# A second Strassen level for the first product of six pairs of convolution cells

## The chip, the cores and the metric

The kernel runs on one core of one Trainium2 chip. The metric is the time of one execution on the device, in microseconds. Five engines work side by side, each through its own queue in order: TensorE (PE in the profile, with its weight loads as PEld), VectorE (DVE), ScalarE (ACT), GpSimd (POOL) and SyncE (SP), which issues nearly all DMAs.

## The reference, cut to what matters

One layer of a decoder trunk on a sequence of 1024 tokens of width 1024, in float32. The part that matters here is the combined input projection of the normalised input `h` (1024 x 1024):

```python
h = rms_norm(x, norm_mix_g[i])
proj = jnp.einsum('bsd,dc->bsc', h, w_in[i])
(q, k, v, z_a, gk_low, cb, cc, xc, z_c, g_a, g_c) = jnp.split(proj, idx, axis=-1)
...
u = causal_dwconv(cc * xc, conv_w[i])
y_c = jnp.einsum('bsc,cd->bsd', (cb * u) * jax.nn.silu(z_c), w_branch_c[i])
```

Each of `cc`, `xc`, `z_c` and `cb` is 1024 columns wide.

## The kernel before, in words

Every large matrix product is cut into *cells*. A cell makes 256 output columns for all 1024 tokens, from a 1024 x 256 block of weights, with one level of Strassen's scheme (seven products in place of eight). The tokens' matrix `h` is cut into quarters, and `hres` holds the seven operands that `h` gives (`hres[0]` to `hres[6]`, each 128 partitions x 4 x 512), made once and kept. A cell streams its own side: `load` fetches the weight quarters (`raw0` to `raw3`, from a ring of 8 tiles), and `prep` makes product k's operand from them on VectorE (the sums are tiles called `T`, from a ring of 4).

Products are made nearly exact in float32 by splitting each operand in two: `split` writes the high part with a ScalarE cast (`hi`) and the low part with a VectorE subtraction (`lo`), and `mm3` then makes three matmuls (hi·hi, hi·lo, lo·hi). The cells' operands lie in a ring of 8 such pairs (`RING = 8`). One product is 4 steps of the contraction x 3 = 12 matmuls whose moving operand is 512 columns wide. A cell uses three PSUM banks, X, Y and V: product 0 goes to X and is copied to Y (ScalarE); product 1 goes to V; products 2, 4 and 6 add to Y, 3 adds to X, 5 adds to V; VectorE and ScalarE take the four output quarters away (`cons`).

There are 40 cells on the weights of `h`, the outputs and the gates, and the sixteen *convolution cells* `cc0, xc0, zc0, cb0, cc1, ... cb3` are among them (four for each group of 256 channels). They run one after the other, all seven products of one cell before the next (`single`). Other cells run in pairs, in which the products of two cells alternate (`pairs`, in the order `PAIR` = 0, 1, 2, 3, 5, 4, 6). `run_groups` walks the list of products, and before it runs one it asks for the loads of the next 14 and the preparation of the next 7.

Nothing of this is issued at once. `Flow` records all operations; `put_in_order` then sets the order on each engine by a list schedule of its own with assumed costs and due times (the main matmuls keep the order of the program), and `emit` issues them. So every instruction of the profile stands at line 507, and instructions are told apart by the names of their tiles: `cc1X<-h0hi,cc1lo` is a matmul of product 0 of cell cc1. Work that fills gaps is woven in by `weave` and `tick` (two ticks for each product): during the convolution cells this is `weights`, which prepares the weights of the last two projections, eight tiles `wt` of 1 MB in two buffers.

After the convolution cells come the gate cells `ga` and `gc` (in pairs, their product 0 was made at the start) with the attention woven in, then `yc`, `ya`, `out` and `gt`. The products 4 and 6 of the last cell `gt3` are made by halves, with a moving operand of 256 columns (`by_halves`).

Of the kernel before, what the change touches and what calls it, by code (L numbers as in the profile page):

```python
# [9 lines left out]
F32 = mybir.dt.float32  # L10
F32R = mybir.dt.float32r
# [3 lines left out]
ALU = mybir.AluOpType  # L15

P = 128
# [8 lines left out]
RING = 8  # L26
# [492 lines left out]
def kernel(  # L519
# [16 lines left out]
    nc = Flow(tc)  # L536
    PS = bass.MemoryType.PSUM
    tt = nc.vector.tensor_tensor
# [3 lines left out]
    def f(ap):  # L542
        return ap.bitcast(F32)
# [85 lines left out]

    def finish_woven():  # L630
        while woven:
            tick()


    def bank(cell, n):
        return psm.tile([P, 512], F32, tag=f"m{3 * cell.set + n}", name=f"{cell.name}{'XYV'[n]}")
# [92 lines left out]

    class Cell:  # L730


        def __init__(self, name, side, src, res, cons, prods=ORDER, begin=None, s1=None, u2=None, s5=None, fresh=(), mixed=False):
            self.name, self.side, self.src, self.res, self.cons = name, side, src, res, cons
            self.prods, self.begin, self.after = list(prods), begin, None
            self.get = {"u2": u2, "s5": s5}
            self.s1, self.seed, self.ready, self.halves = s1, None, lambda k: True, None
            self.raw, self.ring, self.order = [None] * 4, {}, None
            self.steps, self.fresh = ring_steps(name, side, self.raw, fresh, mixed), fresh

        def load(self, k):
            for n in NEED[self.side][k]:
                if self.raw[n] is None and not (self.fresh and k == 1 and n == 3):
                    self.raw[n] = bp.tile([P, 4, P], F32, tag="raw", name=f"{self.name}raw{n}", bufs=8)
                    load(self.raw[n], self.src[n])
            if k == 1 and self.s1 is not None and self.seed is None:
                self.seed = bp.tile([P, 512], F32, tag="raw", name=f"{self.name}s1", bufs=8)
                load(self.seed, self.s1)

        def prep(self, k):  # L750
            if k not in self.ring:
                self.load(k)
                self.ring[k] = self.steps[k]()

        def product(self, k, acc, start):
            self.prep(k)
            shi, slo = self.ring[k]
            rhi, rlo = self.res[k]
            for kt in range(4):
                nc.side = False  # L760
                mm3(acc, shi[:, kt, :], slo[:, kt, :], rhi[:, kt, :], rlo[:, kt, :], start and kt == 0, kt == 3)
                nc.side = True
                if kt % 2 == 1:
                    tick()
# [26 lines left out]
        def run(self, k):  # L791
            if k == self.prods[0]:
                if self.begin:
                    self.begin()
                self.Y = None
            if k == 0:
                self.X = bank(self, 0)
                self.product(0, self.X, True)
                self.Y = bank(self, 1)
                nc.scalar.copy(self.Y, self.X)  # L800
            elif k == 1:
                if self.Y is None:
                    self.Y = bank(self, 1)
                    nc.scalar.copy(self.Y, self.seed)
                self.V = bank(self, 2)
                self.product(1, self.V, True)
                self.c22 = self.taken("s5", self.V)
            elif k == 2:
                self.product(2, self.Y, False)
                self.c12 = self.taken("u2", self.Y)  # L810
                if self.halves:
                    self.Z = psm.tile([P, 512], F32, tag=f"m{3 * (1 - self.set)}", name=f"{self.name}Z")
                    nc.scalar.copy(self.Z[:, 256:], self.Y[:, 256:])
            elif k == 3:
                self.product(3, self.X, False)
                self.cons(0, 0, self.X)
            elif k == 5:
                self.product(5, self.V, False)
                tt(self.c12, self.V, self.c12, op=ALU.add)
                self.cons(0, 1, self.c12)  # L820
            elif k in (4, 6) and self.halves:
                self.by_halves(k)
            elif k == 4:
                self.product(4, self.Y, False)
                tt(self.c22, self.Y, self.c22, op=ALU.add)
                self.cons(1, 1, self.c22)
            elif k == 6:
                self.product(6, self.Y, False)
                self.cons(1, 0, self.Y)
            if self.after:  # L830
                self.after(k)

    def line_up(groups):
        for n, g in enumerate(groups):
            for s, c in enumerate(g):
                c.set = (s if len(g) > 1 else n) % 2
        return [(g[s], k) for g in groups
                for s, k in (g[0].order or [(s, k) for k in g[0].prods for s in range(len(g))])]

    def single(cs):  # L840
        return [[c] for c in cs]

    def pairs(cs):
        for c in cs:
            c.prods = [k for k in PAIR if k in c.prods]
        return [list(cs[n:n + 2]) for n in range(0, len(cs), 2)]

    def run_groups(groups, more=(), ahead=6):


        todo = line_up(groups)
        seq = todo + line_up(more)
        for n, (c, k) in enumerate(todo):
            for reach, what in ((RING + ahead, Cell.load), (RING - 1, Cell.prep)):
                for cc, kk in seq[n:n + reach]:
                    if not cc.ready(kk):
                        break
                    what(cc, kk)
            c.run(k)

    ep = phase("ev")
# [75 lines left out]
    hres = [None] * 7  # L937
# [10 lines left out]
    with phase("prep0") as pool:  # L948
# [75 lines left out]
        at = [0]  # L1024
# [155 lines left out]
    with phase("v", [ph["prep0"]]) as qp:  # L1180
# [76 lines left out]
        qks = []  # L1257
# [4 lines left out]
    with phase("qk", [ph["v"]]) as qp:  # L1262
# [63 lines left out]
        vp = phase("conv", [ph["qk"]])  # L1326
        convs = []
        for g in range(4):
            t, u = [], []
# [35 lines left out]
            for m, cons in (("cc", cc_cons), ("xc", xc_cons), ("zc", zc_cons), ("cb", cb_cons)):  # L1365
                convs.append(Cell(f"{m}{g}", "B", W[f"{m}{g}"], hres, cons, begin=cc_begin if m == "cc" else None))

        run_groups(single(qks), single(convs[:2]))

    with vp:  # L1370
        def weights(vp):


            for w in range(2):
                for kt in range(4):
                    t = vp.tile([P, 4, 512], F32, tag="wt", name=f"wt{w}_{kt}", bufs=2)
                    load(t, wb[w][:, :, kt, :].rearrange("n p c -> p n c"))
                    yield 14
                    b11, b12, b22, b21 = (t[:, n] for n in range(4))
                    if w:  # L1380
                        for n, q in enumerate((b11, b12, b22, b21)):
                            k = kt + 4 * (n >= 2)
                            act(q, q, AF.Copy, scale=gple[:, k:k + 1])
                            if n != 1:
                                store(wtd[w][4 + (n + 1) // 2][:, kt, :], q)
                    tt(b11, b12, b11, op=ALU.subtract)
                    yield 2
                    tt(b12, b22, b12, op=ALU.subtract)
                    yield 2
                    tt(b22, b22, b11, op=ALU.subtract)  # L1390
                    yield 2
                    tt(b21, b21, b22, op=ALU.subtract)
                    for n, q in enumerate((b11, b22, b12, b21)):
                        store(wtd[w][n][:, kt, :], q)
                    yield 4

        gas, gcs = ([Cell(f"{m}{c}", "B", W[f"{m}{c}"], hres, gate_cons(c, bias, dst), prods=(1, 2, 4, 5, 6),
                          s1=s1d[n + c]) for c in range(4)]
                    for n, m, bias, dst in ((0, "ga", bga, gad), (4, "gc", bgc, gcd)))
        weave(weights(vp), 10)  # L1400
        run_groups(single(convs), pairs(gas[:2]))
        finish_woven()

    def attend(hp, ap):
# [456 lines left out]
```

## Time and profile before

| | before |
|---|---|
| median of 3 runs | 1080.68 us (1080.42 to 1080.77) |
| profiled execution, its own time | 1080.98 us |
| its span, first to last instruction | 1079.2 us |
| granted TensorE clock | 0.998 |
| PE / DVE / ACT busy, share of the span | 99% / 81% / 56% |

The page shows one profiled execution. Busy times are sums over the span; the chain that ended last is followed back from the last instruction; a matmul's listed duration runs on after the next one has begun, so the pace of matmuls is read from their starts, or from the chain, which gives consecutive matmuls of one tile with their count and the time they took together.

### The profile page before, as it was taken

Reading aid. Unit: us, or ns where it says so; the run is one execution under the profiler, and the core shown is the slowest. Engines: PE = TensorE matmul, PEld = TensorE weight load, DVE = VectorE, ACT = ScalarE, POOL = GpSimd, SP = SyncE. Lnnn points to the kernel's source line nnn. Section 1 sums busy time; section 2 is a strip of 40 time slices with the busy share of each in tenths; the row PEclk is TensorE's granted clock in tenths of the full one; section 3 lists DMA queues with packets and bytes.
Section 4 is the critical chain, followed back from the end, with each engine's and each line's share of the span. In section 5 each row is a group of like instructions: output and inputs, shape, how many; then the busy total and the mean of one; then the engine's idle time right before and its main releaser. Section 6 shows DMA issues by size and latency. Waiting matters only on the chain.

```text
span 1079.2 us, 14643 instructions
## 1 busy us (share of the span) xinstructions
PE 1069.8 (99%) x4881; PEld 890.8 (83%) x4881; DVE 868.8 (81%) x1353; ACT 605.5 (56%) x1095; POOL 45.5 (4%) x83
## 2 busy tenths in 40 slices
PE   9999999999999999999999999999999999999997
PEld 7887887888888888888888888888888888888886
DVE  6998567678997976857757788887999978889896
ACT  6778538656543455333333367675757635466555
POOL 0000000000000000000000012110000000011021
PEclk9999999999999999999999999999999999999999
DMA  9973564457766598221222689989486878799963
GB/s 315 365 233 105 173 209 142 152 196 233 227 213 220 197 316 266 74 98 49 74 83 69 227 275 310 332 297 333 174 310 234 283 228 297 233 347 339 301 225 139
DMA packets 144828, 239.96 MB, mean 222 GB/s; under 512 B 12016, under 2 KB 57328, under 8 KB 141808
## 3 DMA queue, kind: packets, MB, share of 16 engines
q1 hardware_dynamic: 144608, 238.76, 65.6%
q8 instruction: 38, 0.62, 0.3%
q14 instruction: 38, 0.31, 0.1%
q10 hardware_dynamic: 144, 0.26, 0.1%
HBM read 158.24 MB, written 80.74 MB: 221 GB/s over the span
## 4 chain that ended last, share of the span: by engine, by line
PE 98%; ACT 1%; DVE 0%; issue 0%; POOL 0%; ACTq 0%; DVEq 0%
PE vY L507 3%; PE zaY L507 3%; PE pe L507 2%; PE vX L507 2%; PE zaV L507 2%; PE vV L507 2%; PE op L507 2%; PE zaX L507 2%; PE kv L507 1%; PE ga2Y L507 1%; PE ga0Y L507 1%; PE ga1Y L507 1%; PE ga3Y L507 1%; PE cb3Y L507 1%; PE gc0Y L507 1%; PE xc1Y L507 1%
## 5 line engine op out<-in xcount | busy, mean ns | idle before, releaser
L507 ACT ACT_TABLE_LOAD x20 | 25.7, 1283 | 1.1 <-PEq L1850 0.7
L507 ACT ACTIVATE junk<-x 128x512 bf16<-128x512 f32 (+1 forms) x30 | 18.0, 600 | 12.2 <-DVE x L507 11.8
L507 DVE TENSOR_TENSOR wt<-wt 128x512 f32<-128x512 f32 x32 | 21.7, 687 | 0.3
L507 DVE SCALAR_TENSOR_TENSOR u<-t,vec,u 128x1024 f32<-128x1024 f32 x16 | 20.4, 1278 | 0.0
L507 POOL MEMSET t<- 128x2 f32 x8 | 0.8, 99 | 442.6 <-DMA qkd<-kk 243.7
L507 POOL TENSOR_SCALAR rg<-ms 128x1 f32<-128x1 f32 x8 | 6.4, 796 | 261.4 <-ACT junk L507 261.2
L507 ACT ACTIVATE junk<-op 128x256 bf16<-128x256 f32 x32 | 12.2, 380 | 3.2 <-PE op L507 3.0
L507 ACT CAST S<-S 128x512 fp32r<-128x512 f32 x14 | 8.7, 619 | 9.2 <-PE op L507 8.6
L507 ACT ACTIVATE og<-op,or 128x256 f32<-128x256 f32 x32 | 13.3, 470 | 0.1
L507 ACT ACTIVATE oq<-oq,vec 128x512 f32<-128x512 f32 x20 | 13.1, 715 | 0.0
L507 PE MATMUL pe<-wpehi,pThi 128*128 128x512 f32 x32 | 13.0, 405 | 0.0
L507 PE MATMUL pe<-wpelo,pThi 128*128 128x512 f32 x32 | 13.0, 405 | 0.0
L507 PE MATMUL pe<-wpehi,pTlo 128*128 128x512 f32 x32 | 12.8, 401 | 0.0
L507 PE MATMUL op<-v,aTh 128*128 128x256 f32 x64 | 12.8, 283 | 0.0
L507 DVE TENSOR_TENSOR szl<-og,szl 128x512 f32<-128x512 f32 x16 | 11.0, 688 | 2.1 <-ACT og L507 2.1
L507 POOL TENSOR_TENSOR or<-or,mhalf 128x2 f32<-128x2 f32 x16 | 12.2, 765 | 1.3
L507 DVE SCALAR_TENSOR_TENSOR hq<-hq,vec,rt 128x512 f32<-128x512 f32 x16 | 11.2, 742 | 0.6 <-PE rt L507 0.6
L507 DVE SCALAR_TENSOR_TENSOR S<-S,dds,kv 128x256 f32<-128x256 f32 x24 | 10.4, 475 | 1.5 <-PE kv L507 1.4
L507 DVE TENSOR_TENSOR x<-x,pe 128x512 f32<-128x512 f32 (+1 forms) x18 | 11.2, 629 | 0.3
L507 DVE STREAM_TRANSPOSE oT<-szl 128x512 f32<-128x512 f32 x16 | 11.3, 705 | 0.1
L507 DVE TENSOR_TENSOR u<-u,s 128x512 f32<-128x512 f32 x16 | 10.9, 689 | 0.3
L507 ACT ACTIVATE wt<-wt,vec 128x512 f32<-128x512 f32 x16 | 10.5, 715 | 0.6 <-issue 0.6
(2919 smaller groups left out, 4109.4 us busy)
## 6 DMA issues: line engine op xcount, KB each, us to landing
wtd<-wt SPq DMA_DIRECT2D x44, 256.0 KB, 3.6
wt<-in_wb_dram SPq DMA_DIRECT2D x8, 1024.0 KB, 7.3
v<-vd SPq DMA_DIRECT2D x16, 512.0 KB, 6.1
wgq<-wtd SPq DMA_DIRECT2D x7, 1024.0 KB, 6.5
qk<-qkd SPq DMA_DIRECT2D x12, 512.0 KB, 6.1
vraw<-in_wv_dram SPq DMA_DIRECT2D x20, 256.0 KB, 4.2
zaraw<-in_wv_dram SPq DMA_DIRECT2D x20, 256.0 KB, 3.9
uq<-ud SPq DMA_DIRECT2D x5, 1024.0 KB, 7.3
```

What stands on the lines that cost most here:

```text
L507: o.call(*[place(a) for a in o.args], **{k: place(a) for k, a in o.kw.items()})
```

## The change: what it does

The sixteen convolution cells run in pairs (cc, xc) and (zc, cb). For the last six pairs (groups 1 to 3) the two products 0 of a pair are made together by a new class `Deep`. Both products have the same `hres[0]` on one side, so together they are one product of 512 x 512 weights (two cells' `raw0`, 256 columns each) with 512 x 512 of `h`; `Deep` makes it by a second Strassen level: seven quarter-size products, each 2 steps of the contraction x 3 = 6 matmuls with a moving operand of 256 columns. `h`'s side of the seven operands (`turned`) is made once by `quarters`, woven into the first convolution pairs; one of them is written over a quarter of `hres[0]` once the last cell that needs the plain `hres[0]` (cb0) has made its product 0. The pair's side is made in `Deep.prep` (four half-width sums, four splits, four slots of the ring of 8).

`Deep.run` has four steps, which `line_up` puts between the last products of the pair before: step 0 (two quarter products), product 4 of the second cell, step 1 (two), product 6 of the first cell, step 2 (one), product 6 of the second cell, step 3 (two). Sums of quarter products are made in PSUM: the step's result is copied from one half bank to others by ScalarE (`u`, `X`, and `dw` to SBUF in step 0; `u`'s second half in step 1; `X`'s second half in step 2), and VectorE writes the second cell's X as `u` + `dw` after step 2; the next quarter products add to these. At the end both X are copied to Y, as before.

The `wt` tiles get one buffer instead of two. Cells that are not of these six pairs keep their product 0.

```diff
@@ run (class Cell)
             if k == self.prods[0]:
                 if self.begin:
                     self.begin()
-                self.Y = None
...
+    class Deep:
+        def __init__(self, pair, turned, pool):
+            self.pair, self.turned, self.pool, self.ring = pair, turned, pool, []
+            for c in pair:
+                c.deep, c.prods = self, [k for k in c.prods if k]
+        slots = 4
...
+        def prep(self, k):
...
+            t = [bp.tile([P, 4, P], F32, tag="T", name=f"{name}S{m}", bufs=4) for m in range(2)]
+            s1, s2, s3, s4 = (t[m][:, n:n + 2, :] for m in range(2) for n in (0, 2))
+            tt(s3, a[:, 0:2, :], b[:, 0:2, :], op=ALU.subtract)
+            tt(s1, b[:, 0:2, :], b[:, 2:4, :], op=ALU.add)
+            tt(s2, s1, a[:, 0:2, :], op=ALU.subtract)
+            tt(s4, a[:, 2:4, :], s2, op=ALU.subtract)
+            a11, a12 = put("A", a)
+            s1, s2 = put("S", t[0])
+            s3, s4 = put("T", t[1])
+            a22, = put("B", b[:, 2:4, :])
+            self.ring = [a11, s3, s2, a12, s1, s4, a22]
+
+        def product(self, n, acc, start):
+            shi, slo = self.ring[n]
+            rhi, rlo = self.turned[n]
+            for kt in range(2):
+                nc.side = False
+                mm3(acc, shi[:, kt, :], slo[:, kt, :], rhi[:, kt, :], rlo[:, kt, :], start and kt == 0, kt == 1)
+                nc.side = True
+            tick()
+
+        def run(self, k):
+            self.prep(k)
+            a, b = self.pair
+            left, right = slice(0, 256), slice(256, 512)
+            if k == 0:
+                self.w = pso.tile([P, 512], F32, tag="o", name=f"{a.name}w", bufs=2)
+                self.product(0, self.w[:, left], True)
+                self.product(1, self.w[:, right], False)
+                self.u = pso.tile([P, 512], F32, tag="o", name=f"{a.name}u", bufs=2)
+                a.X = bank(a, 0)
+                nc.scalar.copy(self.u[:, left], self.w[:, left])
+                nc.scalar.copy(a.X[:, left], self.w[:, left])
+                self.d = self.pool.tile([P, 256], F32, tag="dw", name=f"{a.name}dw")
+                nc.scalar.copy(self.d, self.w[:, right])
+            elif k == 1:
+                self.product(2, self.u[:, left], False)
+                nc.scalar.copy(self.u[:, right], self.u[:, left])
+                self.product(3, a.X[:, left], False)
+            elif k == 2:
+                self.product(4, self.u[:, right], False)
+                nc.scalar.copy(a.X[:, right], self.u[:, right])
+                b.X = bank(b, 0)
+                tt(b.X.rearrange("p (n c) -> p n c", n=2), self.u.rearrange("p (n c) -> p n c", n=2),
+                   self.d[:, None, :].to_broadcast([P, 2, 256]), op=ALU.add)
+            else:
+                self.product(5, a.X[:, right], False)
+                self.product(6, b.X[:, left], False)
+                for c in self.pair:
+                    c.Y = bank(c, 1)
+                    nc.scalar.copy(c.Y, c.X)
...
@@ line_up
+            if g[0].deep:
+                for n in range(4):
+                    todo.insert(len(todo) - 3 + n, (g[0].deep, n))
...
@@ the convolution cells
-        run_groups(single(qks), single(convs[:2]))
+        convs = pairs(convs)
+        run_groups(single(qks), convs[:1])
...
-                    t = vp.tile([P, 4, 512], F32, tag="wt", name=f"wt{w}_{kt}", bufs=2)
+                    t = vp.tile([P, 4, 512], F32, tag="wt", name=f"wt{w}_{kt}", bufs=1)
...
+        def quarters(turned):
+            hi, lo = hres[0]
+            th, tl = (vp.tile([P, 3, 2, 256], F32R, name=f"turned{w}") for w in "hl")
...
+            t3 = put(2, apart(2, (1, 1), (0, 1)))
+            yield 1
+            t = apart(0, (0, 1), (0, 0))
+            t1 = put(0, t)
+            yield 1
+            t = less((1, 1), t)
+            t2 = put(1, t)
+            while wide_last[-1].Y is None:
+                yield 1
+            t4 = put(3, less((1, 0), t))
+            b11, b21, b22 = ((at(hi, *a), at(lo, *a)) for a in ((0, 0), (1, 0), (1, 1)))
+            turned += [b11, t3, t2, b21, t1, b22, t4]
+
+        turned = []
+        wide_last = convs[1]
+        for g in convs[2:]:
+            Deep(g, turned, vp)
         weave(weights(vp), 10)
-        run_groups(single(convs), pairs(gas[:2]))
+        weave(quarters(turned), 20)
+        run_groups(convs, pairs(gas[:2]))
```

In `quarters`, `apart` is three VectorE operations on 128 x 512, `less` is two, and each `put` there is one split. In `run_groups` the reach of loads and preparations counts a `Deep` as four slots.

More of the change, by code (lines that the diff above doesn't have):

```diff
@@ L730 @@
     class Cell:
+        slots = 1
         def __init__(self, name, side, src, res, cons, prods=ORDER, begin=None, s1=None, u2=None, s5=None, fresh=(), mixed=False):
@@ L737, in __init__ @@
             self.s1, self.seed, self.ready, self.halves = s1, None, lambda k: True, None
-            self.raw, self.ring, self.order = [None] * 4, {}, None
+            self.raw, self.ring, self.order, self.Y, self.deep = [None] * 4, {}, None, None, None
             self.steps, self.fresh = ring_steps(name, side, self.raw, fresh, mixed), fresh
@@ L831, in run, with ready, load, put @@
                 self.after(k)
+    class Deep:
[4 more added lines that the diff above has]
+        slots = 4
+        def ready(self, k):
+            return True
+        def load(self, k):
+            for c in self.pair:
+                c.load(0)
+        def prep(self, k):
+            if self.ring:
+                return
+            self.load(k)
+            a, b = (c.raw[0] for c in self.pair)
+            name = self.pair[0].name + self.pair[1].name
+            def put(what, src):
+                hi = bp.tile([P, 4, P], F32R, tag="whi", name=f"{name}{what}hi", bufs=RING)
+                lo = bp.tile([P, 4, P], F32R, tag="wlo", name=f"{name}{what}lo", bufs=RING)
+                n = src.shape[1]
+                split(hi[:, 0:n, :], lo[:, 0:n, :], src)
+                return [(hi[:, m:m + 2, :], lo[:, m:m + 2, :]) for m in range(0, n, 2)]
+            t = [bp.tile([P, 4, P], F32, tag="T", name=f"{name}S{m}", bufs=4) for m in range(2)]
[44 more added lines that the diff above has]
+                self.product(6, b.X[:, left], False)
+                for c in self.pair:
+                    c.Y = bank(c, 1)
+                    nc.scalar.copy(c.Y, c.X)
@@ L836, in line_up @@
                 c.set = (s if len(g) > 1 else n) % 2
-        return [(g[s], k) for g in groups
-                for s, k in (g[0].order or [(s, k) for k in g[0].prods for s in range(len(g))])]
+        todo = []
+        for g in groups:
+            if g[0].deep:
+                for n in range(4):
+                    todo.insert(len(todo) - 3 + n, (g[0].deep, n))
+            todo += [(g[s], k) for s, k in (g[0].order or [(s, k) for k in g[0].prods for s in range(len(g))])]
+        return todo
     def single(cs):
@@ L853, in run_groups @@
         for n, (c, k) in enumerate(todo):
-            for reach, what in ((RING + ahead, Cell.load), (RING - 1, Cell.prep)):
-                for cc, kk in seq[n:n + reach]:
-                    if not cc.ready(kk):
+            for reach, what in ((RING + ahead, "load"), (RING - 1, "prep")):
+                met = set()
+                for cc, kk in seq[n:]:
+                    if cc not in met:
+                        reach -= cc.slots
+                    if cc.slots > 1:
+                        met.add(cc)
+                    if reach < 0 or not cc.ready(kk):
                         break
-                    what(cc, kk)
+                    getattr(cc, what)(kk)
             c.run(k)
@@ L1399, with apart, less, put @@
                     for n, m, bias, dst in ((0, "ga", bga, gad), (4, "gc", bgc, gcd)))
+        def quarters(turned):
+            hi, lo = hres[0]
+            th, tl = (vp.tile([P, 3, 2, 256], F32R, name=f"turned{w}") for w in "hl")
+            left, right = slice(0, 256), slice(256, 512)
+            at = lambda t, i, j: t[:, 2 * i:2 * i + 2, (left, right)[j]]
+            tile = lambda n: bp.tile([P, 2, 256], F32, tag="T", name=f"turned{n}", bufs=4)
+            def apart(i, a, b):
+                t, o = tile(i), tile("o")
+                tt(t, f(at(hi, *a)), f(at(hi, *b)), op=ALU.subtract)
+                tt(o, f(at(lo, *a)), f(at(lo, *b)), op=ALU.subtract)
+                tt(t, t, o, op=ALU.add)
+                return t
+            def less(a, t):
+                o = tile("d")
+                tt(o, f(at(hi, *a)), t, op=ALU.subtract)
+                tt(o, o, f(at(lo, *a)), op=ALU.add)
+                return o
+            def put(n, src):
+                h, l = (th[:, n], tl[:, n]) if n < 3 else (at(hi, 0, 1), at(lo, 0, 1))
+                split(h, l, src)
+                return h, l
+            t3 = put(2, apart(2, (1, 1), (0, 1)))
[14 more added lines that the diff above has]
+            Deep(g, turned, vp)
         weave(weights(vp), 10)
-        run_groups(single(convs), pairs(gas[:2]))
+        weave(quarters(turned), 20)
+        run_groups(convs, pairs(gas[:2]))
         finish_woven()
```

## Prediction

> **What bounds the kernel now.** I read the page's head first, then the chain, then the convolution stage by windows.
>
> ```profile
> span 1079.2 us, 14643 instructions
> PE 1069.8 (99%) x4881; PEld 890.8 (83%) x4881; DVE 868.8 (81%) x1353; ACT 605.5 (56%) x1095; POOL 45.5 (4%) x83
> PEclk9999999999999999999999999999999999999999
> PE 98%; ACT 1%; DVE 0%; issue 0%; POOL 0%; ACTq 0%; DVEq 0%
> ```
>
> TensorE is busy for 99% of the span and carries 98% of the chain that ended last, at the full clock all the way. No other engine is near. So a microsecond of matmuls taken out is a microsecond off the end, as long as TensorE doesn't have to wait in exchange; and it has no wait now that could be removed. The stage that is changed, in the windows view (columns: stretch, length, then the busy time of PE, PEld, DVE, ACT, POOL with their instructions, clock, DMA share, GB/s), with three stretches beside it:
>
> ```profile
> 313.00:618.00 305.00, 305.00 (x1349) 252.62 (x1349) 225.26 (x341) 123.34 (x213) 1.42 (x10) 1.00 0.45 150
> 351.00:389.00 38.00, 38.00 (x170) 31.47 (x169) 34.45 (x53) 16.89 (x28) 0.20 (x2) 1.00 0.69 232
> 760.00:850.00 90.00, 90.00 (x399) 74.59 (x398) 86.57 (x114) 60.91 (x91) 0.00 (x0) 1.00 0.71 244
> ```
>
> The sixteen convolution cells run from 313 to 618 us. TensorE is busy for 305.00 of 305.00 us, VectorE for 225.26 (74%), ScalarE for 123.34 (40%). The third row is a stage of the same kind with pairs of cells, where VectorE is busy for 86.57 of 90 us (96%) and TensorE still never waits.
>
> **What the matmuls save.** The pace of wide matmuls is in the chain (start, length, what, how many), that of narrow ones in the timeline of the last cell, whose products 4 and 6 are made by halves (48 matmuls of 256 columns in a row; three of them, with the last wide one ahead):
>
> ```profile
> 389.61 2.72 PE cc1X L507 x12
> 1065.22 0.39 PE L507 MATMUL gt3V<-wg5hi,gt3lo 128*128 128x512 f32 x1
> 1065.45 0.28 PE L507 MATMUL gt3Y<-wg4hi,gt3hi 128*128 128x256 f32 x1
> ...
> 1069.63 0.28 PE L507 MATMUL gt3Y<-wg6hi,gt3lo 128*128 128x256 f32 x1
> 1069.75 0.28 PE L507 MATMUL gt3Z<-wg6hi,gt3hi 128*128 128x256 f32 x1
> ```
>
> A product 0 is 12 matmuls in 2.72 us, 0.2267 us each. From 1065.45 to 1069.63 lie 35 starts of narrow ones: 4.18 / 35 = 0.1194 us each, more than half of 0.2267. A pair loses 24 wide matmuls (24 x 0.2267 = 5.44 us) and gains 7 x 6 = 42 narrow ones. At 0.1194 these are 5.02 us: 0.42 us saved for a pair, 2.55 us for six. But there the narrow ones stand in one long row. In the changed kernel they stand in four groups of 12, 12, 6 and 12 between wide ones, and this the trace shows too, where the attention's narrow matmuls lie among the gate cells' wide ones:
>
> ```profile
> 669.27 1.45 PE op L507 x12
> 670.72 2.52 PE ga2Y L507 x11
> 673.24 2.72 PE ga3Y L507 x12
> ```
>
> Twelve narrow ones took 1.45 us (0.1208 each), and the eleven wide ones behind them 2.52 us where 11 x 0.2267 = 2.49: a change of width costs some 0.03 us (the next twelve are back at 2.72). So a pair costs 42 x 0.1208 + 4 x 0.03 = 5.07 + 0.11 = 5.18 us, 0.26 us less than 5.44; six pairs save 1.55 us. These are the two ends of the matmuls' gain, 1.55 and 2.55 us; I take the first, rounded to 1.6, since it is the row with the new placement.
>
> The Trainium skill ("TensorE: Matmul & The Clock Gate", back-to-back issue gap) gives N / 2.4 + 2.5 ns for a warm matmul. By it 24 wide ones would be an estimated 5.18 us and 42 narrow ones 4.59, six pairs 3.6 us, and the kernel would end near 1077.1; the rows here show 13 ns beside the columns, not 2.5, and they decide.
>
> **What the other engines get, and what hides it.** Durations, from groups of instructions of the stage and of the last cell (`xcount | busy, mean ns | idle before`):
>
> ```profile
> L507 DVE TENSOR_TENSOR xc1lo<-xc1T,xc1hi 128x512 fp32r<-128x512 f32 x4 | 2.8, 690 | 1.8 <-ACT xc1hi L507 1.8
> L507 DVE SCALAR_TENSOR_TENSOR u<-t,vec,u 128x1024 f32<-128x1024 f32 x16 | 20.4, 1278 | 0.0
> L507 DVE TENSOR_SCALAR u<-t,vec 128x1024 f32<-128x1024 f32 x8 | 6.0, 748 | 0.0
> L507 ACT CAST cc2hi<-cc2T 128x512 fp32r<-128x512 f32 x4 | 2.5, 622 | 6.9 <-PE cb1V L507 3.7 <-PE cb1X L507 3.2
> L507 ACT ACTIVATE s<-zc1u 128x512 f32<-128x512 f32 x1 | 0.6, 635 | 1.6 <-DVE zc1u L507 1.6
> L507 ACT COPY gt3Z<-gt3Y x1: 381/381/381, 1060.7 to 1060.7; 128x256 f32<-128x256 f32 x1
> L507 DVE TENSOR_TENSOR gt3s<-gt3Z,gt3s x1: 421/421/421, 1068.7 to 1068.7; 128x256 f32<-128x256 f32 x1
> ```
>
> For a pair VectorE gets four half-width sums (4 x 0.42), one and a half splits more than the two that product 0 had (0.69 + 0.42) and the sum that writes the second X (0.69): 3.5 us. `quarters` adds ten sums and four splits once, 14 x 0.69 = 9.7 us. Six pairs and `quarters` are 30.6 us, and VectorE comes to 256 of some 303 us, 84%. ScalarE gets five copies of 256 (5 x 0.38) and one and a half casts (1.0): 2.9 us for a pair, 20 us with the four casts of `quarters`, 143 of 303 us. Both stay below what the 760 to 850 stretch carries without a wait, so as sums they cost nothing. The tight place is 351 to 389 us, where VectorE has 34.45 of 38 us already and `quarters` and the first pair's preparation (13 us) come down. Its cover is the lead of the preparation:
>
> ```profile
> 371.45 0.69 DVE L507 TENSOR_TENSOR cc1lo<-cc1raw,cc1hi 128x512 fp32r<-128x512 f32 x1
> ```
>
> cc1's first operand is ready 18 us before TensorE starts on cc1 (389.61 above). VectorE may fall back by what it lacks (34.45 + 13 - 38 = 9 us) and still be ahead. If that cover were used up before, it would cost up to those 9 us, once.
>
> The lead does get shorter. A `Deep` holds four of the ring's eight slots until step 3, so the operands around it have 3 to 4 products of lead (some 7 to 9 us) where they had seven (19 us). A cast and a `lo` need 0.62 + 0.69 us after their slot is free. I count nothing for it.
>
> **The new waits.** TensorE waits four times for results of its own that come back through ScalarE: step 1 on step 0, step 2 on step 1, step 3 on step 2, and products 2 on step 3. Between any two lies a full product, 2.72 us. The order of the changed program shows what stands ahead of each copy. Steps 1 and 2 are easy: behind step 0 ScalarE has a cast, a sigmoid (or a copy) and then the copy that is waited for, 0.62 + 0.64 + 0.38 = 1.6 of 2.72 us plus step time. Step 3 is the tightest. In the pairs (cc, xc) the copy of X's second half waits for VectorE's 512-wide sum. From the end of the product ahead of step 2: 0.16 us for the last matmul's result (0.39 - 0.23, from the rows above), a cast 0.62, a `lo` 0.69, the sum 0.69, the copy 0.38 = 2.5 us; TensorE comes to step 3 after 0.72 + 2.72 = 3.44 us. Margin 0.9 us. In the pairs (zc, cb) VectorE has the convolution of xc ahead of that sum (0.75 + 1.28 us): counted from the end of step 1 it is 0.16 + 0.62 + 0.69 + 0.42 + 0.69 + 0.75 + 1.28 + 0.69 + 0.69 = 6.0 us, and the quarter product that reads it starts 2.72 + 0.72 + 2.72 + 0.72 = 6.9 us after that point. Margin 0.9 us again. So no wait, in each of six pairs, but by less than the length of two instructions.
>
> **What else moves.** `wt` has one buffer: SyncE waits for the four stores of one tile before it issues the next load, and the cells' loads queue behind that.
>
> ```profile
> wtd<-wt SPq DMA_DIRECT2D x44, 256.0 KB, 3.6
> wt<-in_wb_dram SPq DMA_DIRECT2D x8, 1024.0 KB, 7.3
> ```
>
> A load is issued, and 14 ticks (about 19 us) later its tile is used; 3.6 + 7.3 = 11 us fit in. The cells' loads behind are held up by 3.6 us, and are needed several products later: nothing, and 3.6 us for a tile if that lead were gone. The order of conv cells in pairs adds no matmul. At the end of the stage zc3 is finished beside cb3, but zc3's last chain (sigmoid and two products, 2.2 us) fits into cb3's last product (2.72 us). POOL has nothing to do with it.
>
> **Sum.** 1080.98 us is the profiled execution's own time (span 1079.2 + 1.8 around it); less 1.6 that is 1079.4. The median of the runs is 0.3 us below that execution, so I forecast 1080.68 - 1.6 = 1079.1 us. With both ends of the matmul cost: 1078.1 to 1079.1; with a few tenths of waits up to 1079.6.
>
> **Rivals.** Some 0.2% (2.16 us) is what a measurement of this kernel can tell from no change, so faster means below 1078.5 and slower above 1082.8.
>
> *Narrow matmuls at their best pace.* If the change of width costs nothing here, six pairs save 2.55 us: 1078.1. For it: the 48 in a row at 0.1194, and that the 0.03 us behind them was seen only in the attention stage, where other things differ. Against it: each of those groups shows it. If width alone set the pace (2.72 / 24 = 0.113), it would be 4.1 us and 1076.6; the row at 0.1194 speaks against that.
>
> *The weight loads become the bound.* 42 loads stand where 24 stood, and a load is listed with 0.19 us:
>
> ```profile
> L507 PEld LDWEIGHTS gt3Z<-wg4hi,gt3hi 128*128 128x128 f32 x4 | 0.8, 192 | 0.0
> ```
>
> One after the other they would take 42 x 0.192 = 8.1 us, 2.6 us more than before: 1096.5. Against it: in that very row of 48 a matmul started each 0.119 us, so loads overlap.
>
> *Waits eat the gain.* At 0.1 to 0.5 us for a pair the time lies between 1079.7 and 1082.1, near no change.
>
> *Step 3 comes late (slower).* If VectorE or ScalarE is one instruction of 1.28 us further behind than the order suggests, each pair's step 3 waits 0.4 us (1.28 - 0.9); if it is two (a convolution in front of the sum and a late `lo`, 2.2 us), 1.3 us. Six times 1.3 less 1.6 is +6.2: 1086.9. It turns to slower from a wait of 0.63 us for a pair ((2.16 + 1.6) / 6). For it: the margins of 0.9 us, the ring with half its lead, a VectorE that must wait for TensorE before nearly each `lo`. Against it: VectorE at 96% made no wait at 760 to 850.
>
> **How the numbers follow.** Forecast (1.6 us saved, 1078.5 to 1079.6): 0.50. Best pace: 0.25, width alone 0.02. Waits eat the gain: 0.10. Step 3 late: 0.12; weight loads: 0.01. Faster takes the best pace, width alone and a little of the forecast's low end, 0.30; slower 0.13; within 0.2% the rest, 0.57. The range 1078.0 to 1082.0 holds the forecast, the best pace and nearly all of the eaten gain; outside are step 3 late, the weight loads and width alone.
>
> **What would show it.** TensorE still busy for all of the stage, and the next gate cell's first product some 1.6 us earlier than at 618 us. In the chain, groups of 12 `w`, 12 `u` and `X`, 6 `u`, 12 `X` at 1.45, 1.45, 0.72 and 1.45 us, and the wide products behind them at 2.72 to 2.75. VectorE near 84% of the stage. I am wrong if the waits list TensorE behind ScalarE or VectorE for X or u, if an issue gap stands in front of step 3, or if the time after the stage changes by itself.

## The result, and the profile after

The changed kernel takes 1078.81 us (median of 21 runs, 1078.32 to 1079.37) against 1080.73 us of the kernel before (21 runs beside them, 1080.23 to 1081.06): ratio 0.9983, interval 0.9977 to 0.9989. It is 1.92 us faster: the interval does not reach 1, but the gain is just inside the 0.2% (2.16 us) below which the prediction called no change. The forecast was 1079.1 us. The profiled execution has its own time of 1078.6 us.

The head of its page and its chain by engine:

```profile
span 1076.8 us, 15006 instructions
PE 1067.4 (99%) x4989; PEld 892.2 (83%) x4989; DVE 894.3 (83%) x1409; ACT 623.4 (58%) x1141; POOL 45.7 (4%) x83
PEclk9999999999999999999999999999999999999999
PE 98%; ACT 1%; DVE 0%; issue 0%; POOL 0%; ACTq 0%; DVEq 0%
```

There are 108 more matmuls (6 x 18) and 2.4 us less of busy TensorE. The convolution stage by windows, in the same stretch as before:

```profile
313.00:618.00 305.00, 305.00 (x1465) 256.94 (x1464) 251.85 (x399) 141.32 (x261) 1.26 (x9) 1.00 0.46 157
```

TensorE is still busy for all of it; VectorE went from 225.26 to 251.85 us, ScalarE from 123.34 to 141.32. All waits of TensorE that the view of waits lists:

```profile
PE warm L507 <- DVE zero L507: 1.4, 1, 1.4
PE zaX L507 <- ACT zax L507: 0.2, 1, 0.2
```

Neither lies in the stage (they stand at 1.4 and 170.6 us), and none is for the `u` or an `X` of a `Deep`. One of the six pairs in the chain (start, length, what):

```profile
380.93 1.42 PE cc1w L507 x12
382.35 2.75 PE cb0Y L507 x12
385.10 0.71 PE cc1u L507 x6
385.81 0.71 PE cc1X L507 x6
386.52 2.75 PE zc0Y L507 x12
389.27 0.71 PE cc1u L507 x6
389.98 2.75 PE cb0Y L507 x12
392.72 0.71 PE cc1X L507 x6
393.44 0.72 PE xc1X L507 x6
394.16 2.75 PE cc1V L507 x12
396.90 2.72 PE xc1V L507 x12
```

The 42 narrow matmuls take 1.42 + 4 x 0.71 + 0.72 = 4.98 us, 0.1186 each, and each of the four wide groups behind them 2.75 instead of 2.72. With those 0.12 us a pair costs 5.10 us where it cost 5.44: 0.34 us saved.

Single times scatter by about half a microsecond, and the traces show one place of it that has nothing to do with the change: cc0's first matmul starts between 312.60 and 313.29 us in the 14 traces of this study, in no order by kernel. I therefore measure the stage by itself, from the first matmul of cc0 to the first of ga0, by their starts in the timeline. What follows it, from there to gt3's product 1 (`gt3V`), is 433.41 us long before and after, and the rest to the end 27.3 and 27.4 us, so nothing is given back later. Each stage below is read from one trace.

| | stage, us | against before |
|---|---|---|
| before | 305.15 | |
| changed kernel | 303.29 | -1.87 |

### The profile page after: what moved, and what is told of

The parts are those of the page before. It is cut to its first block, busy times and chain, and to the rows that moved or that the text cites. A ratio compares the mean times of both kernels' runs of the same rounds, so it can differ in the third digit from the quotient of the medians.

```text
span 1076.8 us, 15006 instructions
## 1 busy us (share of the span) xinstructions
PE 1067.4 (99%) x4989; PEld 892.2 (83%) x4989; DVE 894.3 (83%) x1409; ACT 623.4 (58%) x1141; POOL 45.7 (4%) x83
## 4 chain that ended last, share of the span: by engine, by line
PE 98%; ACT 1%; DVE 0%; issue 0%; POOL 0%; ACTq 0%; DVEq 0%
PE vY L507 3%; PE zaY L507 3%; PE pe L507 2%; PE vX L507 2%; PE zaV L507 2%; PE vV L507 2%; PE op L507 2%; PE zaX L507 2%; PE kv L507 1%; PE ga1Y L507 1%; PE ga3Y L507 1%; PE xc1Y L507 1%; PE xc3Y L507 1%; PE cb2Y L507 1%; PE cb1Y L507 1%; PE xc2Y L507 1%
## 5 line engine op out<-in xcount | busy, mean ns | idle before, releaser
L507 DVE STREAM_TRANSPOSE oT<-szl 128x512 f32<-128x512 f32 x16 | 11.3, 707 | 0.1
L507 POOL TENSOR_SCALAR or<-oms 128x2 f32<-128x2 f32 x16 | 5.8, 363 | 124.8 <-ACT junk L507 124.8
```

Of the source, the lines that this page charges most:

```text
L507: o.call(*[place(a) for a in o.args], **{k: place(a) for k, a in o.kw.items()})
```

## The experiments

**How many pairs.** Three kernels that differ in the number of `Deep` pairs, and the changed kernel again beside them. `pairs_only` leaves out the second level:

```diff
-        for g in convs[2:]:
-            Deep(g, turned, vp)
-        weave(quarters(turned), 20)
```

> The convolution cells go in pairs and the weights' tile has one buffer, as in the changed kernel, but there is no Deep and no quarters: all first products are the 24 wide matmuls of before. Theory (the gain is matmul time alone): 1080.7 us, no change, because the same matmuls stand there in another order. Rival (part of the gain, or a hidden loss, lies in the order by pairs and the single buffer): clearly under 1080.2 or over 1081.2.

`three_pairs`:

```diff
-        wide_last = convs[1]
-        for g in convs[2:]:
+        wide_last = convs[4]
+        for g in convs[5:]:
```

> Only the last three pairs get the second level, quarters are still made once. Theory: each pair is worth 0.34 us (24 x 0.2267 less 42 x 0.1186 and 4 x 0.03), so half of the gain: 1080.7 - 1.0 = 1079.7 us. Rival (a part that is paid once, such as quarters on VectorE, stands against a larger gain of a pair): the line through three and six pairs would not go through 1080.7; with a cost of 1 us paid once, three pairs would give 1080.2.

> The changed kernel once more, on the same chip as the three beside it, as the six-pair point of the series none, three, six, seven. 1078.8 us.

`seven_pairs`:

```diff
-        wide_last = convs[1]
-        for g in convs[2:]:
+        wide_last = convs[0]
+        for g in convs[1:]:
-        weave(quarters(turned), 20)
+        weave(quarters(turned), 4)
```

> The second level for seven pairs instead of six: quarters starts 4 ticks into the stage instead of 20, and only the first pair keeps its wide first products. Theory: one more pair is one more 0.34 us, 1078.8 - 0.34 = 1078.4 us. Rival (VectorE, which must make quarters and the first sums in the first 28 ticks, comes too late): TensorE waits for turned or for the first operands, some 2 to 9 us, 1081 to 1088.

| | median, us | ratio to before, interval | stage, us | against before |
|---|---|---|---|---|
| pairs_only | 1081.08 | 1.0004 (0.9995 to 1.0013) | 305.35 | +0.20 |
| three_pairs | 1080.39 | 0.9995 (0.9987 to 1.0004) | 304.35 | -0.81 |
| six_again | 1078.88 | 0.9982 (0.9973 to 0.9990) | 303.31 | -1.85 |
| seven_pairs | 1080.14 | 0.9996 (0.9987 to 1.0004) | 304.42 | -0.73 |

The stages lie on a line: from none to three pairs -1.00 us, from three to six -1.04 to -1.06, 0.34 us a pair as the chain has it. The medians alone could not show this (that of three_pairs lies 0.4 us above the line, and the intervals are 0.9 us wide to each side). In three_pairs 1.7 to 2.9 us of an execution lie outside the span from first to last instruction, in the other kernels 1.7 to 1.9 us; the medians of the spans, 1079.3, 1078.0 and 1077.1 us for none, three and six pairs, lie on the line within 0.2 us. But the line starts at +0.20, not at zero: the order by pairs costs something. It is one place, where the first matmuls of the attention stand among those of the last cells. PEld in the timeline, before and in pairs_only:

```profile
610.75 0.60 PEld L507 LDWEIGHTS X<-qk 128*128 128x128 f32 x4
```

```profile
602.55 0.52 PEld L507 LDWEIGHTS X<-qk 128*128 128x128 f32 x4 [0.38 <-DVE u L507]
```

In both orders they stand five matmuls behind the last one into `cb3X`, which VectorE then reads (`u<-cb3X,u`). Before, this instruction started 0.42 us behind the start of that last matmul. In the new order VectorE was still at another one (`u<-u,s`) until 601.70 us and started it 0.74 us behind, and the weight load waits for its end at 602.50 us. In the chain the group takes 0.67 us instead of 0.45 (0.71 in the changed kernel). That is the 0.2 us.

seven_pairs did not go on along the line; it lost 1.5 us against it. Its view of waits and VectorE's timeline say where:

```profile
PE xc0Y L507 <- DVE xc0lo L507: 0.9, 1, 0.9
```

```profile
320.71 0.69 DVE L507 TENSOR_TENSOR xc0lo<-xc0raw,xc0hi 128x512 fp32r<-128x512 f32 x1
323.38 1.10 DVE L507 STREAM_TRANSPOSE turned<-kk 128x512 f32<-128x512 f32 x1 [1.98 <-DMA ked<-turned]
327.89 0.69 DVE L507 TENSOR_TENSOR turnedl<-turned,turnedh 128x512 fp32r<-128x512 f32 x1 [3.42 <-ACT turnedh L507]
```

VectorE stands idle for 5.4 us between 321.4 and 327.9, and from 337.6 us on it works without a pause and is late. (The `turned` that the transpose writes is a tile of k1 of the stage before; `turnedl` and `turnedh` are of `quarters`.) My reading: `quarters` writes into memory of the stage before, which is free only behind the transposes of k1; called at 4 ticks, its sums take the four `T` buffers ahead of the cells' own sums, which then wait in line as well. `seven_pairs_later` moves that one number:

```diff
-        weave(quarters(turned), 4)
+        weave(quarters(turned), 11)
```

> Seven pairs with the second level, as in seven_pairs, but quarters starts at 11 ticks instead of 4. In seven_pairs VectorE stood idle from 321.4 to 327.9 us: the sums of quarters had been put in line for the four T buffers, ahead of the cells' own, before the memory of the stage before was free; what it lacked then came out as a wait of 0.9 us for xc0's operand. Theory (with the line free VectorE catches up, and a seventh pair is worth 0.34 us): 1078.5 us, the stage 302.95 us long. Rival (VectorE has too much to do in this pair's time, whatever the order): a wait of 1 us or more stays, 1079.5 to 1082.

The result is 1078.53 us (1078.33 to 1078.91, 11 runs), ratio 0.9979 (0.9971 to 0.9988). The stage is 303.05 us, 0.25 us shorter than with six pairs. The listed wait is gone, but the group of xc0 behind step 0 takes 2.84 us in the chain instead of 2.75, so 0.09 us of the seventh pair's 0.34 is still lost there. This is the fastest version of the study; its median is 0.3 us below that of the changed kernel, which is no more than these medians scatter, so that it is faster rests on the stage's length, in one trace of each. That the listed wait went when one number moved supports the reading; which of the two, the memory or the `T` buffers, held VectorE up was not tried apart.

**Handovers without cover.** `steps_in_a_row` puts the four steps one behind the other:

```diff
-                    todo.insert(len(todo) - 3 + n, (g[0].deep, n))
+                    todo.insert(len(todo) - 1, (g[0].deep, n))
```

> The four steps of a Deep stand directly one behind the other, ahead of the last product of the pair before, with no product between them. Theory (what makes the handovers free is the product that lies between steps): step 1 waits for a copy, 0.05 + 0.36 + 0.1 + what the last matmul's result takes, some 0.7 us; step 2 hardly, because the quarter product into X (0.72 us) covers its copy; step 3 waits for the sum and the copy behind it, 0.7 to 1.4 us. 1.4 to 2.1 us a pair, 8 to 13 us for six: 1087 to 1092, and the waits list TensorE behind ScalarE for u and X. Rival (the second level would be as fast without cover, handovers cost under 0.3 us a pair): under 1080.6.

The result is 1091.72 us, ratio 1.0099 (1.0084 to 1.0114); the stage is 316.34 us, 13.05 us longer than in the changed kernel. Waits of TensorE, for one of the six pairs, and a piece of the chain:

```profile
PE cc1X L507 <- ACT cc1X L507: 0.9, 1, 0.9
PE cc1u L507 <- ACT cc1u L507: 0.4, 1, 0.4
```

```profile
427.44 0.37 ACT zc1u L507
427.80 0.04 issue
427.85 0.98 PE zc1u L507 x6
428.82 0.71 PE zc1X L507 x6
```

The copy stands in the chain itself, and the two waits come in each pair. What a wait costs is read from the starts of the matmuls:

```profile
427.12 0.28 PE L507 MATMUL zc1w<-turnedh,zc1cb1Tlo 128*128 128x256 f32 x1
427.85 0.39 PE L507 MATMUL zc1u<-turnedh,zc1cb1Shi 128*128 128x256 f32 x1 [0.45 <-ACT zc1u L507]
428.07 0.28 PE L507 MATMUL zc1u<-turnedl,zc1cb1Shi 128*128 128x256 f32 x1
```

The wait is listed from the end of the matmul ahead, 0.28 us behind its start, where the next one would have started after 0.12; so the listing leaves out 0.16 us. And the matmul behind the first one starts after 0.22 us (0.19 behind some other waits) instead of 0.12, so that six of them take 0.78 to 0.82 us by their starts instead of 0.71. Together that is some 0.25 us beside each listed wait; the chain, which ends a group with the end of its last matmul, shows both as one, 0.95 to 0.98 us for the six. A pair has three such places, `u`, `X` and the second `X`, where a wait of 0.2 us is listed in five of the six pairs. Listed waits of 1.3 to 1.5 us and 3 x 0.25 are 2.05 to 2.25 us; 13.05 us over six pairs are 2.2. So the products between the steps are worth some 2 us a pair, about six times what the second level brings.

**How thin the cover is.** The sum that writes the second `X` is repeated, without a change of the result (three times here, and five times and twice in two other kernels):

```diff
-                tt(b.X.rearrange(...), self.u.rearrange(...), self.d..., op=ALU.add)
+                for _ in range(3):
+                    tt(b.X.rearrange(...), self.u.rearrange(...), self.d..., op=ALU.add)
```

> The sum that writes the second X is made three times instead of once, with the same result; two more instructions of 0.69 us on VectorE ahead of step 3. In the trace of the changed kernel the second X is ready 1.3 us before its quarter product in the pairs of zc and cb, 2.3 in those of cc and xc. Theory (margin as measured): 1.39 - 1.3 = 0.1 us in three pairs, 1078.8 + 0.3 = 1079.1 us. Rival one (the margin is the 0.9 us that I had worked out): 0.5 us in three pairs, 1080.3. Rival two (VectorE is so full that any addition to it is paid in full): 6 x 1.39 = 8.3 us, 1087.

> The sum that writes the second X is made five times, four more instructions of 0.69 us (2.78 us) ahead of step 3. Theory (a margin of 1.3 us in the pairs of zc and cb; in those of cc and xc 2.3 less the copy of 0.36 us that comes between): waits of 1.5 and 0.9 us, three pairs each, 7.2 us: 1086.0. Rival (there is far more slack than one product, since VectorE is idle for 16% of the stage): under 1080.

Three sums: 1084.21 us, ratio 1.0031 (1.0019 to 1.0042). Five: 1106.26 us, ratio 1.0230 (1.0206 to 1.0254). My expectations of both were wrong, the second by 20 us. The chain of the kernel with three sums has the reason for the first:

```profile
390.99 0.61 DVE xc1X L507
391.60 0.59 DVE s L507
392.19 0.61 DVE xc1X L507
392.80 0.59 DVE u L507
393.38 0.62 DVE xc1X L507
394.01 0.04 issue
394.05 0.98 PE xc1X L507 x6
```

The sums do not stand side by side. VectorE's order puts another instruction between any two, and in a row they start every 0.60 us: the last sum ends 4 x 0.60 = 2.4 us later than the first, not 1.39. The lead it comes from, in the timeline of the changed kernel:

```profile
428.96 0.69 DVE L507 TENSOR_TENSOR cb1X<-zc1u,zc1dw 128x512 f32<-128x512 f32 x1
431.01 0.28 PE L507 MATMUL cb1X<-h0hi,zc1cb1Bhi 128*128 128x256 f32 x1
...
390.40 0.69 DVE L507 TENSOR_TENSOR xc1X<-cc1u,cc1dw 128x512 f32<-128x512 f32 x1
391.13 0.36 ACT L507 COPY cc1X<-cc1u 128x256 f32<-128x256 f32 x1 [0.37 <-DVE xc1X L507]
392.56 0.28 PE L507 MATMUL cc1X<-h0hi,cc1xc1Thi 128*128 128x256 f32 x1
393.27 0.28 PE L507 MATMUL xc1X<-h0hi,cc1xc1Bhi 128*128 128x256 f32 x1
```

For zc and cb the sum ends at 429.65 us and is read at 431.01: 1.36 us (1.22 in the third such pair), of which some 0.14 pass between a sum's end and the matmul behind it where TensorE does wait. So 1.2 us are to spare; for cc and xc it is 2.1 us for the sum, and 1.0 for the copy. 2.4 us of delay against these is 1.2 and 0.3 us; the waits listed are 1.0 to 1.2 us in the three pairs of zc and cb and 0.4 and 0.2 in two of the others, 3.8 us together. The sixth, in the chain above, is too short to be listed (0.11 us), but its six matmuls take 0.98 us all the same. With 0.25 us beside each of the six that is 5.3 us, by which the stage grew.

> The sum that writes the second X is made twice. VectorE's instructions of 512 start every 0.60 us, and one other stands between the two sums, so the second X is ready 1.2 us later. With three sums it was 2.4 us later and TensorE waited 1.0 to 1.2 us in the pairs of zc and cb, 0.2 to 0.4 in two of the others. Theory (the slack of the changed kernel is 1.2 us there, 2.2 in the others): 0 to 0.1 us of wait in three pairs, 1078.8 to 1079.3 us. Rival (what counts is the load of VectorE, not the one instruction's lead): half of what three sums cost, 1081.5 us.

With two sums the delay is 1.2 us, the edge: 1079.42 us, ratio 0.9985 (0.9976 to 0.9995), no listed wait, and the stage is 0.35 us longer than in the changed kernel; `cb1X`'s six matmuls take 0.78 us in the chain instead of 0.72. The median lies 0.1 us above what I expected. The rival, by which the load of VectorE counts and not the one lead, is out: the first 1.2 us of delay in each pair cost 0.35 us in all, the next 1.2 us 4.9 us.

Five sums delay the last by 4.8 us, so waits of 3.6 and 2.7 us were due; 3.4 to 3.6 and 2.5 to 2.6 are listed, 18.1 us together. But the stage is 30.3 us longer, and 0.25 us beside each wait explain 1.5 us of the difference. The timeline of TensorE behind one such wait:

```profile
395.80 0.39 PE L507 MATMUL xc1X<-h0hi,cc1xc1Bhi 128*128 128x256 f32 x1 [2.50 <-DVE xc1X L507]
...
396.85 0.62 PE L507 MATMUL cc1V<-h1lo,cc1hi 128*128 128x512 f32 x1
397.27 0.63 PE L507 MATMUL cc1V<-h1hi,cc1lo 128*128 128x512 f32 x1
...
399.83 0.59 PE L507 MATMUL cc1V<-h1hi,cc1lo 128*128 128x512 f32 x1
400.26 0.39 PE L507 MATMUL cc1V<-h1hi,cc1hi 128*128 128x512 f32 x1
400.49 0.40 PE L507 MATMUL cc1V<-h1lo,cc1hi 128*128 128x512 f32 x1
```

The wide matmuls start every 0.427 us from 396.85 to 400.26, then every 0.23 again: 1.05 us behind the end of a wait of 2.5 us TensorE falls to half its pace for 3.4 us. The granted clock fell with it (last but two in the rows of the windows view; the first row is the 3.41 us ahead):

```profile
393.42:396.83 3.41, 1.03 (x7) 1.01 (x8) 3.41 (x6) 1.04 (x3) 0.00 (x0) 1.00 0.33 112
396.85:400.25 3.40, 3.40 (x9) 2.63 (x8) 3.28 (x6) 0.95 (x2) 0.00 (x0) 0.50 0.58 174
```

Each of the six waits has such a stretch, 3.4 us long in five places and 6.8 in one (437.8 to 444.6 us, 1.0 us of it still waiting). In all, the matmuls behind the waits start 19.1 us late and the slower starts and pace behind them take 11.3 us more, which is the 30.3 to a tenth. The four executions show it as well: with a granted clock of 0.995, 0.991, 0.991 and 0.988 they take 1102.0, 1106.1, 1106.4 and 1108.8 us.

The waits of 1.2 us and less, in the other kernels, have no such stretch behind them. In the 3.41 us ahead of each fall TensorE was busy for 0.8 to 1.5 us; in sum_3_times the least busy 3.41 us of the stage still have 2.2 us, and the clock stays at 1.00. Where between the two the limit lies, and whether it goes by this, was not tried.

**What a change of width costs.** Three kernels made from the one *before*: all 112 products of the convolution cells with some of the four steps of the contraction (`kt`) made by halves of 256 columns, and no `Deep`.

```diff
+                if self.narrow and kt < 2:          # one change
+                if self.narrow and kt % 2 == 0:     # two changes
+                if self.narrow and True:            # all
+                    for cs in (slice(0, 256), slice(256, 512)):
+                        mm3(acc[:, cs], shi[:, kt, :], slo[:, kt, :], rhi[:, kt, cs], rlo[:, kt, cs], ...)
```

> The kernel before, with its convolution cells' products made in part of narrow matmuls: the first two of four kt by halves of 256 columns (12 narrow), the last two wide (6 wide), so one change from narrow to wide in each of 112 products; nothing else is added and there is no handover. Both theories: 12 x 0.1190 + 6 x 0.2267 + 0.03 = 2.82 us for a product instead of 2.72, 112 x 0.10 = 11 us more, 1091.7 us (with a pace of 0.1184: 1090.9).

> As narrow_one_change (1092.2 us), but the first and the third kt are made by halves, so two changes from narrow to wide in each of the 112 products, with the same 12 narrow and 6 wide matmuls. Theory one (each change of width costs a fixed 0.03 us, as the prediction had it): 112 x 0.03 = 3.4 us more, 1095.5 us. Theory two (the starts of the matmuls show it: the first wide ones behind narrow ones come at 233, 236, 228, 233 and 231 ns instead of 227, and the first narrow one behind a wide one at 114 instead of 120; the price builds up with the number of wide ones, up to some ten): two groups of three wide ones cost 2 x 17 ns instead of 27, two early narrow ones give 7 ns back: no difference, 1092 us.

> All 112 products of the convolution cells by halves, 24 narrow matmuls each and no change of width within the stage. Theory (narrow ones have a pace of their own, 0.119 to 0.120 us, wherever they stand): 24 x 0.1194 to 24 x 0.120 = 2.866 to 2.88 us for a product instead of 2.72, 16.4 to 17.9 us more than the 1080.8 of before: 1097 to 1099. Rival (only the change of width costs, the pace is half of the wide one's, 0.1134): no difference from before, 1081.

| | median, us | ratio to before, interval | stage, us | a product |
|---|---|---|---|---|
| one change | 1092.15 | 1.0104 (1.0087 to 1.0121) | 316.27 | +0.099 us |
| two changes | 1091.12 | 1.0097 (1.0083 to 1.0111) | 315.55 | +0.093 us |
| all narrow | 1098.94 | 1.0169 (1.0155 to 1.0183) | 322.99 | +0.159 us |

(The last column is the stage's growth over 112.) One product of each in the chain, in this order:

```profile
400.83 2.82 PE cc1X L507 x18
```

```profile
400.25 2.81 PE cc1X L507 x18
```

```profile
402.68 2.88 PE cc1X L507 x24
```

Narrow matmuls in an endless row take 2.88 / 24 = 0.1200 us; the rival, by which they cost half a wide one, is out. By the formula of the Trainium skill ("TensorE: Matmul & The Clock Gate", back-to-back issue gap), which the page gives for a matmul taken by itself, it would be an estimated 256 / 2.4 + 2.5 = 109 ns; 120 were measured. And two changes of width in a product cost no more than one, but 0.7 us less over the stage. So there is no fixed price of a change: 0.03 us for each would have made it 3.4 us more. In the timeline of the first kernel the six wide matmuls behind narrow ones take 1.39 us (402.10 to 403.49), 0.03 more than 6 x 0.2267, and in the second three take 0.69 (400.80 to 401.49), 0.01 more than 3 x 0.2267: the price builds up over the wide ones that follow. It ends there: in the changed kernel the twelve behind a group cost 0.03 us, the next twelve none.

## Why the prediction was right, point by point

*What bounds the kernel.* Right: a microsecond of matmuls taken out came off the end. The stage lost 1.87 us, the time 1.92, what follows it kept its length.

*The matmuls' gain.* Right in kind, too small: 0.26 us a pair foreseen, 0.34 measured, 2.05 instead of 1.55 us for six. The mis-sized term is the pace of narrow matmuls, 0.1208 from the attention's row where the groups here have 0.1186; over 42 that is 0.09 us a pair. The 0.03 us of a change of width was the right amount here, where twelve wide ones follow each group, but the wrong reading: it belongs to the wide matmuls behind the change, not to the change. The rival of the best pace (2.55 us) was nearer on the narrow ones and wrong to leave the 0.03 out.

*"The order of conv cells in pairs adds no matmul."* True, and yet it costs 0.20 us by what it does to the attention's first matmuls. I had looked at the cells alone and not at what is placed between them. The two errors have opposite signs, so that the forecast came out nearer than its terms is luck: 2.05 - 0.20 = 1.85 us against 1.6.

*The other engines.* Right: VectorE 251.85 us for 256, ScalarE 141.32 for 143, and no wait. VectorE's is lower since I added durations of 0.69 us where instructions in a row start every 0.60.

*The new waits.* Right that there is none. The margin of 0.9 us stands against 1.0 (the copy, in cc and xc) and 1.2 us (the sum, in zc and cb) measured. That the cover is needed is shown by steps_in_a_row, and its thickness by the three kernels with more sums.

*Step 3 late, the rival on the slow side.* It did not happen, but it was near: one more instruction of VectorE there, with what the order puts beside it, costs 0.35 us, two cost 5.3 us. Its total was too high (six waits of 1.3 us, 7.8 us, for a delay of 2.2; measured 5.3 for 2.4), because the margin is 1.2 us in three pairs and 2.1 in the others, not 0.9 in all. The price of a single wait was too low: I had taken a wait at its length, and beside what is listed come 0.25 us, and behind 2.5 us of waiting 3.4 us at half the pace.

*Weight loads as the bound.* Out: 24 loads and matmuls in 2.88 us.

*The ring's shorter lead and the single buffer of `wt`.* No wait in the changed kernel. In pairs_only, which has the single buffer too, the whole 0.20 us is accounted for elsewhere. The ring's lead was not tried by itself; seven_pairs shows that it can run out where VectorE is held up.

## What to carry to other kernels

When one engine is busy all the time, a second Strassen level pays by the paces of the two widths, and those are to be taken from starts of matmuls of that width in the same kind of group: 0.1186, 0.1200 and 0.1208 us differ by over a quarter of the gain (0.09 of 0.34 us a pair). The handovers cost nothing here with a full product between the steps and some 2 us a pair with none (nothing between was tried); look at the one instruction that ends last and what its engine's order may put ahead of it, not at how busy that engine is. And where a change reorders the work, see also what stands woven into it.

## What the runs showed of the hardware that I had not expected

- A wait of TensorE costs some 0.25 us more than it is listed with: 0.16 us lie ahead of what is counted, and behind waits of 0.1 to 1.2 us the next six narrow matmuls took 0.78 to 0.82 us by their starts instead of 0.71.
- After waits of 2.5 to 3.6 us the granted clock stood at 0.50 for 3.4 us, once for 6.8; after the first of them the wide matmuls started every 0.427 us instead of 0.227, eight times. The Trainium skill ("TensorE: Matmul & The Clock Gate", What's actually happening) has a half clock of 1.2 GHz after at least one idle window of about 3.4 us, left again after about as long a busy one; the pace of 0.427 us (512 / 1.2) and the length of the slow stretch agree with it, but 2.5 us of waiting were enough here, with TensorE busy for 1.03 of the 3.41 us ahead.
- Wide matmuls behind narrow ones come some 2% slower for the first six (1.39 us instead of 1.36), and two groups of three pay less than one of six.
- VectorE's sums of 128x512 are listed with 0.69 us and start every 0.60 us in a row.
